# A fused streaming-encoder step: attention scores of a head pair on the two row halves of TensorE

## The chip, the cores and the metric

The kernel runs on one core of a Trainium2 chip. Its time is device microseconds (us) of one execution of the whole program. Of the runs shown the median is 2116.94 us (three runs, 2116.49 to 2117.7). TensorE multiplies and is the only writer of PSUM, VectorE (DVE) and ScalarE (ACT) read PSUM and work on SBUF, GpSimd (POOL) issues stores and does small SBUF work, and SP issues loads.

## The reference, cut to what matters

The reference is one layer of a conformer-like encoder on 1024 prompt frames and 64 sample frames, 1024 features, 16 heads of 64. What the change touches is the attention:

```python
h = rms_norm(x, norm_mix)
glu_a, glu_b, q, k, v, gates = jnp.split(h @ w_in, SPLITS, axis=-1)
# each frame attends to its own chunk of 64 and the 8 chunks before it, head by head (HEAD_DIM = 64)
sc = jnp.einsum("bnqhd,bnkhd->bnhqk", qc, band_k).astype(jnp.float32) * (dh ** -0.5)
sc = sc + rel_bias(rel_table, dist)
pr = jax.nn.softmax(sc, axis=-1).astype(v.dtype)
o = jnp.einsum("bnhqk,bnkhd->bnqhd", pr, band_v).reshape(b, s, h * dh)
```

Beside it stand a GLU, a causal depthwise convolution of width 31 with a layernorm, gates, an output projection, a channel mixer (up, convolution of width 3, GELU, down) and a per-layer input embedding.

## The kernel before

Features lie on the 128 partitions, frames along the free dimension. Each projection is a *job*: 128 output features of all 1088 frames, in three groups of 384, 384 and 320 columns. A product of float32 precision is made of three fp32r products: every operand is split into a high part (rounded to fp32r) and a low part (the rest), and high x high, high x low and low x high add up in PSUM (`mm3`, lines 154 to 166: eight blocks of the contraction, three matmuls each, so 24 matmuls a group). `split_into` (L168) makes the two parts: the high one with an ACT copy (L170), the low one with a DVE instruction (L171).

In the first long stage (up to about 916 us of the trace) the jobs follow each other in the order `order_1a`: for each of the eight pairs of heads i the jobs q, k, v, then three or four fill jobs (GLU value and gate, branch gates). The attention of pair i is threaded through those jobs. `job_group` calls `tick` twice a group: as the hook of `mm3`, after half of the 24 matmuls, and again after the group's evacuation `evac`. After a job's first group `w_ahead` splits the next job's weights (ACT L134, then DVE L135).

Attention works in 9 steps p a pair: 8 blocks of 128 queries against n = 128, 256, 384, 512 and then 640 keys, and one of the 64 sample queries against 576 keys. `pipe` has one entry a head and step, 18 for a pair, and each `tick` takes one:

- `step_S` (L463) computes the scores of one head. To use all 128 rows of the array with heads of 64 features, q and k are stored stacked: tile `Q[h]` holds the high part of q twice, `K[h]` the high part of k in one half of the partitions and the low part in the other, and `ql[h]` the low part of q over zeros. Two products (L481 with `Q`, L483 with `ql`) then give all three terms. 640 and 576 keys are done in two column halves. `tensor_tensor_reduce` (L487, DVE) adds the bias and takes the minimum, out of PSUM. The score tile has two PSUM banks, one buffer.
- `step_E` (L495, ACT) exponentiates and sums; one tick later DVE inverts the sum (L553) and `step_R` (L517, ACT) scales.
- `step_T` (L504) transposes the probabilities in blocks of 128 on TensorE, in another two PSUM banks, one buffer; ACT copies them out (L507).
- `step_PV` (L528) multiplies with v for both heads of a pair at once, head 0 on the left half of the array's columns and head 1 on the right half; `step_AT` splits the result and stores it.

Inside a tick the order on each engine is that of the program: `step_S`, `step_R` of the head before, background work, `step_PV`, `step_T`, `step_E`, background work. The background work (`bg_tick`) is the depthwise convolution's taps on DVE (L327), later the layernorm on DVE and ACT; a tick may do it in proportion to the TensorE time that it counts (`spent`, `RATIO`).

The evacuation of a q group is four ACT copies (L683) and two DVE instructions (L688), of 64 partitions each; that of a k group is two ACT copies (L696) and two DVE instructions (L708), and the cached keys take two and two (L601, L605). A projection has two PSUM buffers, so the group after the next one waits for this evacuation. PSUM's eight banks are: projections 2, scores 2, transposes 2, `o_ps` 1, small sums 1.

Of the kernel before, what the change touches and what calls it, by code (L numbers as in the profile page):

```python
# [9 lines left out]
F32 = mybir.dt.float32  # L10
# [65 lines left out]
def encoder_step(ctx: ExitStack, tc: tile.TileContext, I, O):  # L76
# [143 lines left out]
    with tc.manual_schedule():  # L220
# [55 lines left out]
        ps_s = att.enter_context(tc.tile_pool(name="ps_s", bufs=1, space=PSUM))  # L276
        ps_t = att.enter_context(tc.tile_pool(name="ps_t", bufs=1, space=PSUM))
# [4 lines left out]
        hsq = [at.tile([P, KW], F32, tag=f"K{h}", name="hsq") for h in range(2)]  # L282
# [174 lines left out]
        ql = [at.tile([P, T], F32R, tag=f"QL{h}", name="QL") for h in range(2)]  # L457
        for h in range(2):
            nc.gpsimd.memset(ql[h][64 - 64 * h:128 - 64 * h, :].bitcast(F32), 0.0)
        pipe = []  # L460
        stages = {"e": [], "t": [], "pv": []}

        def step_S(st):  # L463
# [11 lines left out]
            st.update(m=m, n=n, vb=(8 if smp else k0 // P), q0=q0)  # L475
# [9 lines left out]
            s = at.tile([P, 640], F32, tag="s", name="s", bufs=3)  # L485
            sm = at.tile([P, 3], F32, tag="sm", name="sm", bufs=6)
            nc.vector.tensor_tensor_reduce(  # L487
                out=s[0:m, 0:n].rearrange("p (x c) -> p x c", x=nh), in0=ps[0:m, 0:nh, 0:w],
                in1=c["bias"][h][0:m, b0:b0 + n].rearrange("p (x c) -> p x c", x=nh),
                scale=1.0, scalar=3e38, op0=ALU.add, op1=ALU.min, accum_out=sm[0:m, 0:1])  # L490
            st.update(s=s, sm=sm)

        def step_E(st):
            m, n, s, sm = st["m"], st["n"], st["s"], st["sm"]
            nc.scalar.activation(out=s[0:m, 0:n], in_=s[0:m, 0:n], func=AF.Exp, scale=-1.0, bias=sm[0:m, 0:1],  # L495
                                 accum_out=sm[0:m, 1:2])

        def step_T(st):
            m, n, s = st["m"], st["n"], st["s"]
            nb = (n + P - 1) // P  # L500
            ps = ps_t.tile([P, 1024], F32, tag="t", name="t_ps")
            for b in range(nb):
                w = min(P, n - b * P)
                nc.tensor.transpose(ps[0:w, b * P:b * P + m], s[0:m, b * P:b * P + w], ident[0:m, 0:m])  # L504
            pt = at.tile([P, 640], F32, tag="pt", name="pt", bufs=2)
            if m == P:
                nc.scalar.activation(out=pt[:, 0:n], in_=ps[:, 0:n], func=AF.Copy)  # L507
            else:
                nc.scalar.activation(out=pt[:, 0:512].rearrange("p (b q) -> p b q", q=P)[:, :, 0:m],
                                     in_=ps[:, 0:512].rearrange("p (b q) -> p b q", q=P)[:, :, 0:m], func=AF.Copy)  # L510
                nc.scalar.activation(out=pt[0:64, 512:512 + m], in_=ps[0:64, 512:512 + m], func=AF.Copy)
            st.update(pt=pt, nb=nb)

        def step_R(st):

            m, n, s, sm = st["m"], st["n"], st["s"], st["sm"]
            nc.scalar.activation(out=s[0:m, 0:n], in_=s[0:m, 0:n], func=AF.Copy, scale=sm[0:m, 2:3])  # L517

        def step_PV(pair):

            st = pair[0]
            c, m, n, nb = cur[st["i"]], st["m"], st["n"], st["nb"]
            o_ps = ps_o.tile([P, 512], F32, tag="o", name="o_ps")
            for b in range(nb):
                w = min(P, n - b * P)
                for x in pair:
                    a = 64 * x["h"]
                    nc.tensor.matmul(o_ps[a:a + 64, 0:m], lhsT=c["v"][0:w, st["vb"] + b, a:a + 64],  # L528
                                     rhs=x["pt"][0:w, b * P:b * P + m], start=(b == 0), stop=(b == nb - 1))
            st["o"] = o_ps  # L530

        def step_AT(st):
            m = st["m"]
            aT = at.tile([P, 2, P], F32R, tag="aT", name="aT")
            split_into(aT, 0, m, st["o"][:, 0:m])
# [4 lines left out]
        def tick(base=1.95):  # L540
# [3 lines left out]
            pair = len(stages["pv"]) == 2  # L544
            late = len(stages["t"]) > 1 or (stages["t"] and not pipe)
            if pair:
                spent += 0.218 * stages["pv"][0]["nb"] + 0.2
            if late:
                spent += 0.107 * ((stages["t"][0]["n"] + P - 1) // P)
            if pipe:  # L550
                spent += 0.5
            for x in stages["e"]:
                nc.vector.reciprocal(out=x["sm"][0:x["m"], 2:3], in_=x["sm"][0:x["m"], 1:2])  # L553
            new = pipe.pop(0) if pipe else None
            if new is not None:
                step_S(new)
            for x in stages["e"]:
                step_R(x)
            stages["e"].clear()
            bg_tick(RATIO * spent, 1)  # L560
            if pair:
                step_PV(stages["pv"])
                step_AT(stages["pv"][0])
                stages["pv"].clear()
            if late:
                st = stages["t"].pop(0)
                step_T(st)
                stages["pv"].append(st)
            if new is not None:
                step_E(new)  # L570
                stages["e"].append(new)
                stages["t"].append(new)
# [23 lines left out]
        def kv_cache(i):  # L596
            c = cur[i]
            kc = kc_t.pop(i)
            for h in range(2):
                a = 64 * h  # L600
                nc.scalar.activation(out=c["K"][h][a:a + 64, SEQ:SEQ + PAST], in_=kc[a:a + 64, 0:PAST], func=AF.Copy)  # L601
            for h in range(2):
                a, b = (0, 64) if h == 0 else (64, 0)
                kt = c["K"][h]
                nc.vector.tensor_tensor(out=kt[b:b + 64, SEQ:SEQ + PAST], in0=kc[a:a + 64, 0:PAST],  # L605
                                        in1=kt[a:a + 64, SEQ:SEQ + PAST].bitcast(F32), op=ALU.subtract)
# [14 lines left out]
        def job_begin(kind, i):  # L621
            hl = w_use()
            if kind == "q":
                cur[i] = {"Q": [at.tile([P, T], F32R, tag=f"Q{h}", name="Q") for h in range(2)]}
                kc_load(i)
                load_head(i)
            if kind == "k":
                if i < 7:
                    bias_rows(i + 1)
                cur[i]["K"] = [at.tile([P, KW], F32R, tag=f"K{h}", name="K") for h in range(2)]  # L630
# [17 lines left out]
        def evac(kind, i, g, ps):  # L648
# [28 lines left out]
                elif kind == "q":  # L677
                    c = cur[i]
                    for b in (0, 64):
                        for h in range(2):  # L680
                            a = 64 * h
                            o = a if b == 0 else 64 - a
                            nc.scalar.activation(out=c["Q"][h][o:o + 64, c0:c0 + n], in_=ps[a:a + 64], func=AF.Copy,  # L683
                                                 scale=-0.125)
                    for h in range(2):
                        a = 64 * h
                        q = c["Q"][h]
                        nc.vector.scalar_tensor_tensor(out=ql[h][a:a + 64, c0:c0 + n], in0=ps[a:a + 64],  # L688
                                                       scalar=-0.125, in1=q[a:a + 64, c0:c0 + n].bitcast(F32),
                                                       op0=ALU.mult, op1=ALU.subtract)  # L690
                elif kind == "k":
                    c = cur[i]
                    for h in range(2):
                        a = 64 * h
                        for o, w, d in segs(c0, n, 0, SEQ + PAST):
                            nc.scalar.activation(out=c["K"][h][a:a + 64, d:d + w], in_=ps[a:a + 64, o:o + w],  # L696
                                                 func=AF.Copy)
# [6 lines left out]
                    for h in range(2):  # L704
                        a, b = (0, 64) if h == 0 else (64, 0)
                        kt = c["K"][h]
                        for o, w, d in segs(c0, n, 0, SEQ + PAST):
                            nc.vector.tensor_tensor(out=kt[b:b + 64, d:d + w], in0=ps[a:a + 64, o:o + w],  # L708
                                                    in1=kt[a:a + 64, d:d + w].bitcast(F32), op=ALU.subtract)
                elif kind == "v":  # L710
# [21 lines left out]
                    if g == 2:  # L732
                        for p in range(9):
                            for h in range(2):
# [929 lines left out]
```

## Time and profile before

| what | value |
|---|---|
| median of the runs shown | 2116.94 us (2116.49 to 2117.7) |
| the profiled execution's own time | 2115.92 us |
| its span, first to last instruction | 2114.1 us |
| TensorE busy | 2078.1 us (98%) |
| VectorE busy | 1361.7 us (64%) |
| ScalarE busy | 881.6 us (42%) |
| granted TensorE clock, mean | 0.993 |
| share of TensorE in the chain that ended last | 88% |

The profile records every instruction of one execution. A matmul's row holds its time from start to modelled end; matmuls are pipelined, so the distance between the starts of two of them, not the duration, says what one costs. A wait is put down to the event that came last.

### The profile page before, as it was taken

To read this page: it belongs to the slowest core of one execution; us is meant where nothing else is said; L and a number is where in the kernel's file an instruction comes from. 1 tells how busy PE (TensorE), PEld (TensorE's weight loads), DVE (VectorE), ACT (ScalarE), POOL (GpSimd) and SP (SyncE) were. 2 spreads that over 40 slices of the span, in tenths; PEclk is the share of its full clock that TensorE was granted. 3 is DMA by queue.
4 is the path that set the end of the run, shared out by engine and by line. 5 is a ranking of instruction groups with operands and counts; after the bars stand their busy time and mean duration, and the time that the engine had idled before them with its cause. 6 is when DMAs were issued, how large, how long until landed. Compare 5 with 4: busy or idle time off the path is not lost.

```text
span 2114.1 us, 35321 instructions
## 1 busy us (share of the span) xinstructions
PE 2078.1 (98%) x14472; PEld 2024.5 (96%) x14472; DVE 1361.7 (64%) x2310; ACT 881.6 (42%) x1695; POOL 228.2 (11%) x455
## 2 busy tenths in 40 slices
PE   8999999999999999999999999999999999999997
PEld 6999999999999999899999998999999999999997
DVE  6887878777877755542354577777777753345644
ACT  5564737365746475850122344333333331123421
POOL 5110101111111011110000000000000020000400
PEclk9999999999999999999999999999999999999998
DMA  3313121212221321235343232121212173240011
GB/s 133 118 41 98 63 91 59 99 61 87 74 78 52 104 78 67 69 127 190 138 143 105 90 122 82 62 92 62 92 62 93 51 284 112 70 133 34 20 51 55
DMA packets 64705, 192.51 MB, mean 91 GB/s; under 512 B 8368, under 2 KB 22976, under 8 KB 63200
## 3 DMA queue, kind: packets, MB, share of 16 engines
q1 hardware_dynamic: 43072, 104.00, 14.6%
q0 software_dynamic: 21328, 85.71, 11.3%
q8 instruction: 113, 1.85, 0.4%
q10 hardware_dynamic: 144, 0.56, 0.1%
q14 instruction: 48, 0.39, 0.1%
HBM read 146.18 MB, written 54.01 MB: 95 GB/s over the span
## 4 chain that ended last, share of the span: by engine, by line
PE 88%; DVE 4%; ACT 4%; issue 2%; DMA 1%; POOL 0%; POOLq 0%; SPq 0%; DVEq 0%; ACTq 0%
PE pj L159 16%; PE pj L161 15%; PE pj L160 15%; PE pj L1173 7%; PE pj L1174 7%; PE pj L1172 7%; PE pj L1474 3%; PE pj L1475 3%; PE pj L1473 3%; PE o_ps L528 3%; PE t_ps L504 3%; PE s_ps L481 1%; PE s_ps L483 1%; DVE acc L1019 1%; ACT tmp L1018 0%
## 5 line engine op out<-in xcount | busy, mean ns | idle before, releaser
L159 PE MATMUL pj<-hT,whl 128*128 128x384 f32 (+1 forms) x1296 | 440.5, 340 | 3.6 <-DVE QL L688 2.2
L161 PE MATMUL pj<-hT,whl 128*128 128x384 f32 (+1 forms) x1296 | 424.9, 328 | 0.3 <-DVE whl L135 0.3
L160 PE MATMUL pj<-hT,whl 128*128 128x384 f32 (+1 forms) x1296 | 424.1, 327 | 0.0
L327 DVE SCALAR_TENSOR_TENSOR c<-u,cc,c 128x1118 f32<-128x1118 f32 x240 | 330.9, 1379 | 2.8
L159 PEld LDWEIGHTS pj<-hT,whl 128*128 128x128 f32 x1296 | 243.6, 188 | 8.6 <-issue 5.4
L161 PEld LDWEIGHTS pj<-hT,whl 128*128 128x128 f32 x1296 | 243.6, 188 | 0.6 <-DVE whl L135 0.6
L160 PEld LDWEIGHTS pj<-hT,whl 128*128 128x128 f32 x1296 | 243.9, 188 | 0.0
L1172 PE MATMUL pj<-mp,wq 128*128 128x272 f32 x704 | 204.0, 290 | 5.0 <-ACT ug L1248 2.7
L1174 PE MATMUL pj<-mp,wq 128*128 128x272 f32 x704 | 204.5, 290 | 0.0
L1173 PE MATMUL pj<-mp,wq 128*128 128x272 f32 x704 | 204.2, 290 | 0.0
L134 ACT ACTIVATE whl<-raw 128x1024 fp32r<-128x1024 f32 (+3 forms) x100 | 100.3, 1003 | 222.4 <-PE pj L1475 134.6
L1149 ACT ACTIVATE wq<-raw 128x512 fp32r<-128x512 f32 x144 | 84.2, 625 | 191.7 <-DVE raw L1158 135.6
L135 DVE TENSOR_TENSOR whl<-raw,whl 128x1024 fp32r<-128x1024 f32 (+3 forms) x100 | 115.7, 1158 | 62.5 <-ACT whl L134 62.1
L487 DVE CUSTOM_DVE_ANT_0 s<-s_ps,bias 128x640 f32<-128x640 f32 (+3 forms) x144 | 95.2, 661 | 81.5 <-PE s_ps L483 78.2
L1474 PE MATMUL pj<-gp,whl 128*128 128x384 f32 (+1 forms) x432 | 141.2, 327 | 0.3 <-DVE gp L1383 0.3
L1475 PE MATMUL pj<-gp,whl 128*128 128x384 f32 (+1 forms) x432 | 141.1, 327 | 0.0
L1473 PE MATMUL pj<-gp,whl 128*128 128x384 f32 (+1 forms) x432 | 141.0, 326 | 0.0
L1172 PEld LDWEIGHTS pj<-mp,wq 128*128 128x128 f32 x704 | 133.8, 190 | 5.4 <-ACT ug L1248 2.9
L1173 PE MATMUL pj<-bq,wq 128*128 128x272 f32 x480 | 138.5, 288 | 0.0
L1174 PE MATMUL pj<-bq,wq 128*128 128x272 f32 x480 | 138.3, 288 | 0.0
L1172 PE MATMUL pj<-bq,wq 128*128 128x272 f32 x480 | 138.1, 288 | 0.0
L1173 PEld LDWEIGHTS pj<-mp,wq 128*128 128x128 f32 x704 | 133.9, 190 | 0.0
(258 smaller groups left out, 4794.1 us busy)
## 6 DMA issues: line engine op xcount, KB each, us to landing
raw<-in_w_in SPq DMA_DIRECT2D x56, 512.0 KB, 3.2
raw<-in_w_ffn_up SPq DMA_DIRECT2D x44, 512.0 KB, 4.2
q_d<-ug POOLq DMA_DIRECT2D x22, 544.0 KB, 3.0
gp<-q_d POOLq DMA_DIRECT2D x22, 544.0 KB, 6.6
tg<-s_d POOLq DMA_DIRECT2D x16, 544.0 KB, 3.9
aP<-a_d POOLq DMA_DIRECT2D x8, 1088.0 KB, 6.0
a_d<-aT POOLq DMA_DIRECT2D x64, 128.0 KB, 2.2
f_d<-e_d POOLq DMA_DIRECT2D x16, 383.5 KB, 5.1
```

The lines of the kernel that those rows point to most:

```text
L134: nc.scalar.activation(out=hl[:, 0, 0:k, :], in_=raw[:, 0:k, :], func=AF.Copy)
L135: nc.vector.tensor_tensor(out=hl[:, 1, 0:k, :], in0=raw[:, 0:k, :], in1=hl[:, 0, 0:k, :].bitcast(F32), op=ALU.subtract)
L159: nc.tensor.matmul(ps, lhsT=wsel(hl, 0, k), rhs=r[:, 0, c0:c0 + n], start=(k == 0), stop=False)
L160: nc.tensor.matmul(ps, lhsT=wsel(hl, 0, k), rhs=r[:, 1, c0:c0 + n], start=False, stop=False)
L161: nc.tensor.matmul(ps, lhsT=wsel(hl, 1, k), rhs=r[:, 0, c0:c0 + n], start=False, stop=(k == K - 1))
L327: nc.vector.scalar_tensor_tensor(out=c_t[f], in0=u_t[f][:, j:j + CCOL], scalar=pc("conv_dw", f * CW + j), in1=c_t[f], op0=ALU.mult, op1=AL ...
L1172: nc.tensor.matmul(ps, lhsT=q[:, 0, kt, :], rhs=h, start=start and kt == 0, stop=False)
L1173: nc.tensor.matmul(ps, lhsT=q[:, 0, kt, :], rhs=l, start=False, stop=False)
L1174: nc.tensor.matmul(ps, lhsT=q[:, 1, kt, :], rhs=h, start=False, stop=stop and kt == 3)
L1473: nc.tensor.matmul(ps, lhsT=hl[:, 0, k, :], rhs=h, start=k == 0, stop=False)
L1474: nc.tensor.matmul(ps, lhsT=hl[:, 0, k, :], rhs=l, start=False, stop=False)
L1475: nc.tensor.matmul(ps, lhsT=hl[:, 1, k, :], rhs=h, start=False, stop=k == K - 1)
```

## The change

q and k are no longer stacked. `Q` and `K` are tiles of two planes, high and low, with head 0 on partitions 0 to 63 and head 1 on 64 to 127, as the projection leaves them; `ql` and its zeros are gone. The evacuation of q is `split_into` (one ACT copy, one DVE instruction on 128 partitions), that of k and of the cached keys one ACT copy and one DVE instruction for each stretch.

`step_S` now does both heads of a step. For each column half it issues three products (high x high, low x high, high x low) for each head, each with 64 rows of contraction: those of head 0 on the upper row half of the array, those of head 1 on the lower, alternating, into different PSUM banks. The scores of both heads take four banks. The transposes of both heads take the same four banks: scores and transposes are two tiles of one buffer (`tag="st"`, one buffer), so the scores of a step wait until the copies of the transposes before them are done, and the transposes wait until both reductions of the scores before them are done.

`pipe` has 9 entries a pair. Ticks alternate (`turn`): an even tick (the hook in a group's middle) does `step_S` of a new step, background work, `step_PV` of an older one, `step_E`; an odd tick (after a group's evacuation) does background work, `step_T` of both heads, the two inversions and the two `step_R` of the step just exponentiated. `spent` counts 1.1 for a pair's scores in place of 0.5 for a head's. During the start of the kernel the four banks belong to a pool `ps_h` that is closed before the first attention. The score tiles `s` in SBUF have four buffers in place of three.

```diff
@@ step_S
-            i, p, h = st["i"], st["p"], st["h"]
+            i, p = st["i"], st["p"]
...
-            ps = ps_s.tile([P, 2, 512], F32, tag="s", name="s_ps")
+            ps = ps_st[0].tile([P, 2, 2, 512], F32, tag="st", name="s_ps")
             wm = max(w, 256)
             for x in range(nh):
                 a = k0 + x * w
-                nc.tensor.matmul(ps[0:m, x, 0:wm], lhsT=c["Q"][h][:, q0:q0 + m], rhs=c["K"][h][:, a:a + wm],
-                                 start=True, stop=False)
-                nc.tensor.matmul(ps[0:m, x, 0:wm], lhsT=ql[h][:, q0:q0 + m], rhs=c["K"][h][:, a:a + wm],
-                                 start=False, stop=True)
...
+                for j, (sq, sk) in enumerate(((0, 0), (1, 0), (0, 1))):
+                    for h in range(2):
+                        r = slice(64 * h, 64 * h + 64)
+                        nc.tensor.matmul(ps[0:m, h, x, 0:wm], lhsT=c["Q"][r, sq, q0:q0 + m],
+                                         rhs=c["K"][r, sk, a:a + wm], start=(j == 0), stop=(j == 2))
+            st["s"], st["sm"] = [], []
+            for h in range(2):
+                s = at.tile([P, 640], F32, tag="s", name="s", bufs=4)
+                sm = at.tile([P, 3], F32, tag="sm", name="sm", bufs=6)
+                nc.vector.tensor_tensor_reduce(
+                    out=s[0:m, 0:n].rearrange("p (x c) -> p x c", x=nh), in0=ps[0:m, h, 0:nh, 0:w],
...
@@ step_T
-            ps = ps_t.tile([P, 1024], F32, tag="t", name="t_ps")
+            ps = ps_st[0].tile([P, 2, 1024], F32, tag="st", name="t_ps")
+            st["pt"] = []
+            for h, s in enumerate(st["s"]):
+                for b in range(st["nb"]):
+                    w = min(P, n - b * P)
+                    nc.tensor.transpose(ps[0:w, h, b * P:b * P + m], s[0:m, b * P:b * P + w], ident[0:m, 0:m])
+                pt = at.tile([P, 640], F32, tag="pt", name="pt", bufs=2)
+                if m == P:
+                    nc.scalar.activation(out=pt[:, 0:n], in_=ps[:, h, 0:n], func=AF.Copy)
...
@@ tick
+            odd = turn[0]
+            turn[0] = 1 - odd
+            new = done = flip = None
+            if not odd:
+                if pipe:
+                    new = pipe.pop(0)
+                    spent += 1.1
+                if stages["pv"]:
+                    done = stages["pv"].pop(0)
+                    spent += 0.218 * done["nb"] + 0.2
+            elif stages["t"]:
+                flip = stages["t"].pop(0)
+                spent += 0.214 * flip["nb"]
             if new is not None:
                 step_S(new)
             bg_tick(RATIO * spent, 1)
+            if done is not None:
+                step_PV(done)
             if new is not None:
                 step_E(new)
                 stages["e"].append(new)
+            if flip is not None:
+                step_T(flip)
+                stages["pv"].append(flip)
+            if odd:
+                for st in stages["e"]:
+                    for sm in st["sm"]:
+                        nc.vector.reciprocal(out=sm[0:st["m"], 2:3], in_=sm[0:st["m"], 1:2])
+                    step_R(st)
+                    stages["t"].append(st)
+                stages["e"].clear()
...
@@ evac, kind q
-                    for b in (0, 64):
-                        for h in range(2):
...
+                    split_into(c["Q"], c0, n, ps, scale=-0.125)
@@ evac, kind k
+                    kt = c["K"]
+                    for o, w, d in segs(c0, n, 0, SEQ + PAST):
+                        nc.scalar.activation(out=kt[:, 0, d:d + w], in_=ps[:, o:o + w], func=AF.Copy)
...
+                    for o, w, d in segs(c0, n, 0, SEQ + PAST):
+                        nc.vector.tensor_tensor(out=kt[:, 1, d:d + w], in0=ps[:, o:o + w],
+                                                in1=kt[:, 0, d:d + w].bitcast(F32), op=ALU.subtract)
...
         for p in range(9):
-                            for h in range(2):
-                                pipe.append({"i": i, "p": p, "h": h})
+                            pipe.append({"i": i, "p": p})
```

## Rows read from the trace of the kernel before

**Rows 1.** Page, part 1: busy time, share of the span, instructions of each engine

```profile
PE 2078.1 (98%) x14472; PEld 2024.5 (96%) x14472; DVE 1361.7 (64%) x2310; ACT 881.6 (42%) x1695; POOL 228.2 (11%) x455
```

**Rows 2.** Busy time by stretch: the attention, and the end of it

```profile
88.00:916.00 828.00, 820.09 (x5834) 780.75 (x5833) 601.51 (x969) 492.44 (x1049) 99.51 (x192) 1.00 0.22 74
...
855.00:915.00 60.00, 56.55 (x433) 51.09 (x432) 34.25 (x64) 52.13 (x91) 8.64 (x14) 1.00 0.17 57
```

**Rows 3.** TensorE in time, one tick: start, us, line, tiles, shape, count

```profile
340.14 0.31 PE L481 MATMUL s_ps<-K,Q 128*128 128x320 f32 x1
...
340.59 0.31 PE L483 MATMUL s_ps<-K,QL 128*128 128x320 f32 x1
340.83 1.09 PE L528 MATMUL o_ps<-pt,v 128*64 128x128 f32 x16
341.85 0.77 PE L504 MATMUL t_ps<-ident,s 128*128 128x128 f32 x5
342.37 0.39 PE L159 MATMUL pj<-hT,whl 128*128 128x320 f32 x1
342.60 0.31 PE L160 MATMUL pj<-hT,whl 128*128 128x320 f32 x1
```

**Rows 4.** First pair of PV products alone; then four weight loads of PV

```profile
340.83 0.33 PE L528 MATMUL o_ps<-pt,v 128*64 128x128 f32 x2
...
341.21 0.25 PEld L528 LDWEIGHTS o_ps<-pt,v 128*64 128x64 f32 x4
```

**Rows 5.** TensorE in time, scores of one head over 512 columns

```profile
330.04 0.39 PE L481 MATMUL s_ps<-K,Q 128*128 128x512 f32 x1
330.27 0.39 PE L483 MATMUL s_ps<-K,QL 128*128 128x512 f32 x1
```

**Rows 6.** TensorE in time, around instructions of 64 rows (the sample step)

```profile
373.74 0.34 PE L161 MATMUL pj<-hT,whl 128*128 128x384 f32 x1
374.00 0.52 PE L504 MATMUL t_ps<-ident,s 64*128 64x64 f32 x5
374.46 0.45 PE L159 MATMUL pj<-hT,whl 128*128 128x384 f32 x1
374.74 0.34 PE L160 MATMUL pj<-hT,whl 128*128 128x384 f32 x1
...
377.63 0.44 PE L159 MATMUL pj<-hT,whl 128*128 128x384 f32 x1
377.91 0.33 PE L160 MATMUL pj<-hT,whl 128*128 128x384 f32 x1
```

**Rows 7.** Groups by shape, 88 to 916: busy us, mean ns, idle before

```profile
L528 PEld LDWEIGHTS o_ps<-pt,v 128*64 128x64 f32 x1088 | 56.5, 136 | 19.5 <-issue 14.7 <-ACT pt L507 3.2 <-DVE sm L553 0.8
L517 ACT ACTIVATE s<-s,sm 128x640 f32<-128x640 f32 x64 | 52.9, 827 | 32.2 <-DVE sm L553 32.2
L507 ACT ACTIVATE pt<-t_ps 128x640 f32<-128x640 f32 x64 | 44.8, 700 | 14.4 <-PE t_ps L504 14.3
L481 PEld LDWEIGHTS s_ps<-K,Q 128*128 128x128 f32 x192 | 36.0, 188 | 1.3 <-DVE sm L487 1.3
L688 DVE SCALAR_TENSOR_TENSOR QL<-pj,Q 64x384 fp32r<-64x384 f32 x28 | 15.5, 555 | 37.2 <-ACT Q L683 36.9
```

**Rows 8.** All engines in time, a tick after a weight split

```profile
337.51 1.23 DVE L135 TENSOR_TENSOR whl<-raw,whl 128x1024 fp32r<-128x1024 f32 x1 [1.45 <-ACT whl L134]
337.61 0.60 PE L504 MATMUL t_ps<-ident,s 128*128 128x128 f32 x4
...
338.73 0.81 DVE L487 CUSTOM_DVE_ANT_0 s<-s_ps,bias 128x640 f32<-128x640 f32 x1
339.46 1.38 DVE L327 SCALAR_TENSOR_TENSOR c<-u,cc,c 128x1118 f32<-128x1118 f32 x1
```

**Rows 9.** Waits of TensorE's projections in 88 to 916: us, times, longest

```profile
PE pj L159 <- DVE QL L688: 2.2, 2, 1.6
...
PE pj L159 <- DVE K L708: 0.7, 1, 0.7
```

More of the change, by code (lines that the diff above doesn't have):

```diff
@@ L280, in encoder_step @@
         misc[0] = ps_m
-        hsq = [at.tile([P, KW], F32, tag=f"K{h}", name="hsq") for h in range(2)]
+        head = ExitStack()
+        ps_h = head.enter_context(tc.tile_pool(name="ps_h", bufs=1, space=PSUM))
+        ps_st = [None]
+        hsq2 = at.tile([P, 2, KW], F32, tag="K", name="hsq")
+        hsq = [hsq2[:, h] for h in range(2)]
         hd = {}
@@ L456, in encoder_step @@
         cur = {}
-        ql = [at.tile([P, T], F32R, tag=f"QL{h}", name="QL") for h in range(2)]
-        for h in range(2):
-            nc.gpsimd.memset(ql[h][64 - 64 * h:128 - 64 * h, :].bitcast(F32), 0.0)
         pipe = []
         stages = {"e": [], "t": [], "pv": []}
+        turn = [0]
         def step_S(st):
-            i, p, h = st["i"], st["p"], st["h"]
+            i, p = st["i"], st["p"]
             c = cur[i]
@@ L493, in step_E @@
         def step_E(st):
-            m, n, s, sm = st["m"], st["n"], st["s"], st["sm"]
-            nc.scalar.activation(out=s[0:m, 0:n], in_=s[0:m, 0:n], func=AF.Exp, scale=-1.0, bias=sm[0:m, 0:1],
-                                 accum_out=sm[0:m, 1:2])
+            m, n = st["m"], st["n"]
+            for s, sm in zip(st["s"], st["sm"]):
+                nc.scalar.activation(out=s[0:m, 0:n], in_=s[0:m, 0:n], func=AF.Exp, scale=-1.0, bias=sm[0:m, 0:1],
+                                     accum_out=sm[0:m, 1:2])
@@ L498, in step_T @@
         def step_T(st):
-            m, n, s = st["m"], st["n"], st["s"]
-            nb = (n + P - 1) // P
-            ps = ps_t.tile([P, 1024], F32, tag="t", name="t_ps")
[L502 to L511, printed above, removed]
@@ L514, in step_R, with step_PV @@
         def step_R(st):
[L516 to L521, printed above, removed]
+            m, n = st["m"], st["n"]
+            for s, sm in zip(st["s"], st["sm"]):
+                nc.scalar.activation(out=s[0:m, 0:n], in_=s[0:m, 0:n], func=AF.Copy, scale=sm[0:m, 2:3])
+        def step_PV(st):
             c, m, n, nb = cur[st["i"]], st["m"], st["n"], st["nb"]
@@ L525, in step_PV @@
                 w = min(P, n - b * P)
-                for x in pair:
-                    a = 64 * x["h"]
+                for h in range(2):
+                    a = 64 * h
                     nc.tensor.matmul(o_ps[a:a + 64, 0:m], lhsT=c["v"][0:w, st["vb"] + b, a:a + 64],
[L529 to L533, printed above, removed]
+                                     rhs=st["pt"][h][0:w, b * P:b * P + m], start=(b == 0), stop=(b == nb - 1))
             aT = at.tile([P, 2, P], F32R, tag="aT", name="aT")
-            split_into(aT, 0, m, st["o"][:, 0:m])
+            split_into(aT, 0, m, o_ps[:, 0:m])
             dma_st(out=a_d[st["i"]][:, :, st["q0"]:st["q0"] + m], in_=aT[:, :, 0:m].bitcast(F32))
@@ L543, in tick @@
             spent = base
[L544 to L554, printed above, removed]
+            odd = turn[0]
[11 more added lines that the diff above has]
+                spent += 0.214 * flip["nb"]
             if new is not None:
                 step_S(new)
-            for x in stages["e"]:
-                step_R(x)
-            stages["e"].clear()
             bg_tick(RATIO * spent, 1)
[L561 to L568, printed above, removed]
+            if done is not None:
+                step_PV(done)
             if new is not None:
@@ L598, in kv_cache @@
             kc = kc_t.pop(i)
-            for h in range(2):
[L600 to L606, printed above, removed]
+            kt = c["K"]
+            nc.scalar.activation(out=kt[:, 0, SEQ:SEQ + PAST], in_=kc[:, 0:PAST], func=AF.Copy)
+            nc.vector.tensor_tensor(out=kt[:, 1, SEQ:SEQ + PAST], in0=kc[:, 0:PAST],
+                                    in1=kt[:, 0, SEQ:SEQ + PAST].bitcast(F32), op=ALU.subtract)
         kc_t = {}
@@ L623, in job_begin @@
             if kind == "q":
-                cur[i] = {"Q": [at.tile([P, T], F32R, tag=f"Q{h}", name="Q") for h in range(2)]}
+                cur[i] = {"Q": at.tile([P, 2, T], F32R, tag="Q", name="Q")}
                 kc_load(i)
@@ L629, in job_begin @@
                     bias_rows(i + 1)
-                cur[i]["K"] = [at.tile([P, KW], F32R, tag=f"K{h}", name="K") for h in range(2)]
+                cur[i]["K"] = at.tile([P, 2, KW], F32R, tag="K", name="K")
                 kv_cache(i)
@@ L678, in evac @@
                     c = cur[i]
-                    for b in (0, 64):
[L680 to L690, printed above, removed]
+                    split_into(c["Q"], c0, n, ps, scale=-0.125)
                 elif kind == "k":
                     c = cur[i]
[L693 to L697, printed above, removed]
+                    kt = c["K"]
+                    for o, w, d in segs(c0, n, 0, SEQ + PAST):
+                        nc.scalar.activation(out=kt[:, 0, d:d + w], in_=ps[:, o:o + w], func=AF.Copy)
                     if g == 1:
@@ L808, in begin @@
             parts[g] = norm_parts([xt[f][:, c0:c0 + n] for f in range(KT)], "norm_mix", hd[g], n, hT, c0,
-                                  lambda: at.tile([P, 640], F32, tag="s", name="hn", bufs=3), HDVE[g])
-            two = ps_s.tile([P, 2, 512], F32, tag="s", name="pj") if g == 1 else None
+                                  lambda: at.tile([P, 640], F32, tag="s", name="hn", bufs=4), HDVE[g])
+            two = ps_h.tile([P, 2, 512], F32, tag="w", name="pj") if g == 1 else None
             for x, kind in enumerate(("gb", "ga")):
@@ L883, in encoder_step @@
         xt = None
+        head.close()
+        ps_st[0] = att.enter_context(tc.tile_pool(name="ps_st", bufs=1, space=PSUM))
         for kind, i in order_1a[2:-1]:
```

38 lines of the change are left out of this document (15 added, 23 removed).

## The prediction

> **What bounds the kernel now.** I read the page's part 1 first: TensorE is busy 98% of the span, the next engine 64% [rows 1]. Then the busy time by stretch: in the attention, 88 to 916 us, TensorE is busy 820.09 of 828 us at a granted clock of 1.00 (2.4 GHz), DVE 601.51, ACT 492.44 [rows 2]. So every us that TensorE's stream gets shorter or longer there is a us of the kernel, and a wait of another engine counts only where TensorE stands still. The exception is the end of the stage, 855 to 915, where ACT is busy 52.13 of 60 us and TensorE already loses 3.45 [rows 2]. Busy time does not say what a matmul costs, since matmuls overlap; so the third view is TensorE in time, where the reader takes distances between starts [rows 3 to 6].
>
> **The products: what is saved.** A score product of 320 columns follows the one before it after 0.15 us (340.14 to 340.59 is three distances), one of 512 after 0.23 [rows 3, 5]: 0.457 ns a column. A head has 256+256+384+512+4x640+576 = 4544 score columns in its nine steps (short steps are padded to 256). Before, a pair streams 2 heads x 2 products x 4544 columns = 8.31 us. After, it streams 3 products x 4544 = 6.23 us if the two heads run side by side. That is 2.08 us a pair, **-16.6 us** for eight.
>
> Do they run side by side? No row of before has two row halves at work. The nearest are the PV products, which use two column halves: the first two together take 0.33 us, hardly more than one score product's 0.31 [rows 4], and 16 of them, of some 0.27 us each, pass in 1.02 (340.83 to 341.85) [rows 3]. Their weight loads overlap too: four loads of 136 ns are through in 0.25 us [rows 4, 7], which is two distances of 0.11 apart plus one load. I take the same for row halves. The bounds: fully side by side as above, or one after the other, 12 products where 8 stood, which is 8.31 x 0.5 x 8 = +33.2 us in place of -16.6.
>
> **What is added: changes of the array's shape.** The sample step's transposes have 64 rows, and the rows around them show what it costs to leave the full array and to come back. From the last projection product (373.74) to the second one behind the transposes (374.74) pass 1.00 us; two products of 384 columns (0.175 each) and five short transposes (half of the 0.104 of a full one [rows 3], say 0.06 each) are 0.65 of it, so 0.35 is lost: 0.09 before the first transpose (0.26 instead of 0.175), 0.05 in its own start, and 0.21 on the way back, half of it in the first product, whose weights were not loaded ahead (374.46 to 374.74 is 0.28 instead of 0.175) [rows 6]. The same 0.28 stands behind a PV step that goes straight back to projections [rows 6]. Into PV it is 0.24 instead of 0.147 plus 0.05 [rows 3], 0.14; from PV to a transpose 1.02 - 8 x 0.109 - 0.05 for the entry, plus 0.055 in the first transpose, 0.155 in all [rows 3]. Full transposes after projections or scores of the full array, and back, cost nothing extra.
>
> So a score step on row halves, now entered from projections, costs about 0.20 to enter: 0.09 for the drain and 0.105 for a first load of 128 fp32r columns like the projections' (188 ns against 136 for PV's 64 columns [rows 7]). The bounds for it are 0.09 (drain alone) and 0.21 (the way back). Per pair of heads:
>
> - after: 9 entries into scores x 0.20, 7 score to PV x 0.14, 2 scores to projections (no PV yet) x 0.20, 2 projections to PV x 0.14, 9 PV to projections x 0.20, one visit to the sample's transposes 0.35: 1.80 + 0.98 + 0.40 + 0.28 + 1.80 + 0.35 = 5.61 us;
> - before: 9 entries into PV x 0.14, 8 PV to transposes x 0.155, the last PV to projections 0.20, the sample's transposes twice (one entered out of PV, so 0.21 + 0.35): 1.26 + 1.24 + 0.20 + 0.56 = 3.26 us.
>
> The difference is 2.35 us a pair, **+18.8 us** for eight. The halved scores sit between two changes each time, and before they were the same shape as the projections: that is why the saving is eaten.
>
> **Evacuations.** q falls from four ACT copies and two DVE instructions a group to one and one, k from two and two to one and one. TensorE waited 2.2 + 0.7 us in three places for the second of the two DVE instructions [rows 9]; without it each release comes 0.555 us earlier [rows 7]: **-1.7 us**. The rest of this relief is hidden under TensorE's stream.
>
> **The shared banks.** Now the transposes wait for both reductions of the step before, and the next scores for both copies. Queued behind a waiting transpose or score on TensorE stands the whole projection stream.
>
> *Scores to transposes.* The window is the PV step (1.02 to 1.3), the way back and 12 projection products (12 x 0.175 = 2.1): 3.3 us. Two reductions need 2 x 0.73 (338.73 to 339.46) and perhaps the rest of a convolution tap of 1.38 before them [rows 8]: 2.9. That fits by little. It does not always fit behind a weight split: there L135 stood idle 1.45 us for ACT's half and held the reduction back to 338.73, 1.1 us after the scores had streamed and the transposes behind them began (337.61) [rows 8]. In the new order two scalings of 0.83 [rows 7] stand ahead of ACT's half, and they wait for inversions that stand behind a tap. I count from the end of the transposes: a copy 0.7, two scalings 1.7, ACT's half 1.05, L135 1.22, 4.7 us; the scores end 3.2 after the same point; so the reductions start 1.5 late and need 1.5: 3.0 of 3.3, and a tap ahead of the inversions makes 4.4, 1.1 too many. Two such ticks a pair, 16 in all, between 0 and 1.1 each; I take a quarter us, as the tap is in front in some of them: **+4 us** (0 to 18).
>
> *Transposes to scores.* The window is 2.1 us (1.8 in a short group), two copies of 0.70 [rows 7] with ACT free take 1.4: hidden. At the end of the stage, where ACT has almost no slack [rows 2], a layernorm instruction in front makes it late; I allow four misses of half a us, **+2** (0 to 8; an allowance, not a row).
>
> **The sum**, against the profiled execution's 2115.92 us: -16.6 + 18.8 - 1.7 + 4 + 2 = +6.5, 2122.4. The median of the runs shown is 1.0 above that execution, so I say 2123.4, rounded to **2123 us**: 0.3% slower. A difference under 0.2% (4.2 us) can hardly be told from none here.
>
> **Rivals.**
>
> *Faster: entering the row halves costs only the drain.* If the first loads of both halves go on under the drain, each entry is 0.09 and not 0.20: 72 x 0.11 = -7.9; with that slack the shared banks may cost nothing: -6. Then 2109.5 us. For it: the short transposes' entry cost only 0.14 [rows 6]. Against: the return rows show a first load in the open every time [rows 6]. It decides from about 10.5 us below my sum on (below 2112.7); neither half alone does it.
>
> *No change.* The waits on the banks stay hidden and an entry costs what the transposes' did (0.14, -4.3): 2113 to 2121, middle 2117. For it: in the whole attention the scores' weight loads waited only 1.3 us for reductions [rows 7].
>
> *Slower: the loads of the two row halves go one after the other.* 188 against 136 ns for 128 and 64 columns is 0.81 ns a column [rows 7], so 0.104 a load and 0.208 a pair of loads, above the 0.147 of 320 columns, the 0.175 of 384 and the 0.117 of 256. Per pair of heads 24 x 0.061 + 3 x 0.033 + 6 x 0.091 = 2.1 us, +16.9: 2140. Against it: PV's loads overlap [rows 4].
>
> The Trainium skill, "TensorE: Matmul & The Clock Gate", section "Measured speedup vs the span model", has four row tiles run 3.07 times as fast as one after the other, not 4. No run here shows it yet. By that share two tiles would run 1.54 times as fast, an estimate from that page: twelve products of 12.46 us a pair would take 8.1, the saving would be 1.7 us and the sum 2138. I give it part of the chance of this rival, as PV's pairs show no such loss.
>
> *The change does not do what it says: the halves take turns.* Then 2123 + 49.8 = 2173 us. Against it: rows 4.
>
> **Chances.** My forecast (more than 0.2% slower, side by side) 0.40, no change 0.28, faster 0.20, loads in turn 0.08, halves in turn 0.04. So faster 0.20, same 0.28, slower 0.52. The range takes in the first four with the bank waits at half their upper bounds and leaves out the last: 2109 to 2141. The forecast's own range is 2119 to 2135.
>
> **What would show it.** In the new trace: six distances of about 0.147 us in a 640-key step of both heads, two products in each (right) or twelve (halves in turn) or six of 0.21 (loads in turn). A gap of 0.26 between the last projection product and the first score, and 0.28 in the first projection product behind PV, 18 times a pair where the latter stood twice or less. No wait for QL or K. Waits of transposes on the reduction (L487's new line) in the group behind a weight split, at most 1.1 us, and of scores on the copies near 900. The prediction is wrong if the waits on the shared banks come in every tick, since DVE is then the clock of the stage, or if the change of shape is not paid at all.

## The result and the profile after

The changed kernel takes 2202.1 us (median of six runs, 2199.4 to 2203.78), the kernel before in the same session 2116.72. The ratio is 1.0406, 95% interval 1.0391 to 1.042: 4.1% slower. The forecast was 2123 us, range 2109 to 2141. One of the six runs of the kernel before was slow (2868.01 us) and stands in that median, while the ratio compares fast runs alone. The direction was right; the time lies 61 us above the range, and none of the rivals gave it.

The page of the changed kernel, parts 1 and 4 (the counterpart of [rows 1]; in part 4 the shares of the chain that ended last):

```profile
span 2197.3 us, 35659 instructions
PE 2094.6 (95%) x14696; PEld 2012.2 (92%) x14696; DVE 1320.1 (60%) x2246; ACT 829.8 (38%) x1583; POOL 224.2 (10%) x453
...
PE 82%; ACT 7%; DVE 5%; issue 4%; DMA 1%; POOL 0%; SPq 0%; POOLq 0%; ACTq 0%; DVEq 0%
```

TensorE has 16.5 us more of busy time, but the span is 83.2 us longer: TensorE stands still, which it hardly did before. No other engine is busier than before. The busy time by stretch says where, with the attention now ending at 1003 us (counterpart of [rows 2]; columns: stretch, its length, busy us and instructions of PE, PEld, DVE, ACT, POOL, granted clock, DMA share, GB/s):

```profile
88.00:1003.00 915.00, 841.93 (x6078) 772.19 (x6078) 564.92 (x914) 448.04 (x952) 99.60 (x193) 0.99 0.20 67
```

This stretch is 87 us longer than that of [rows 2], and idle time of TensorE in it rose from 7.91 to 73.07 us. Who is waited for stands in the waits of TensorE from 88 to 1010 us (the counterpart of [rows 9]; waiting line, what it waits for, us in total, times, longest):

```profile
PE t_ps L511 <- ACT pt L514: 66.8, 64, 4.4
PE t_ps L511 <- ACT pt L519: 5.1, 8, 0.6
PE v_ps L708 <- ACT lnb L384: 1.2, 2, 0.6
PE pj L159 <- ACT sg L677: 0.7, 1, 0.7
```

64 + 8 is 72, the number of steps: in every step, once, the transposes wait for ACT's copy of transposes, 71.9 us in all. No wait of TensorE's products for q, k, a reduction or the scores' banks is left. One step in time shows which copy it is (all engines' rows of the two lines; the last column is the idle time before and its releaser):

```profile
364.08 0.60 PE L511 MATMUL t_ps<-ident,s 128*128 128x128 f32 x4
...
364.78 0.60 ACT L514 ACTIVATE pt<-t_ps 128x512 f32<-128x512 f32 x1
...
365.43 0.66 PE L511 MATMUL t_ps<-ident,s 128*128 128x128 f32 x4 [0.75 <-ACT pt L514]
...
366.18 0.60 ACT L514 ACTIVATE pt<-t_ps 128x512 f32<-128x512 f32 x1 [0.81 <-PE t_ps L511]
```

The first four transposes are head 0's. Its copy runs from 364.78 to 365.38, and head 1's transposes start 0.05 after it. It is the copy of the *same step*, not of the step before. `step_T` takes one tile of four banks for both heads, and in the program's order head 0's copy out of that tile stands ahead of head 1's transposes into it.

The score and PV products of the tick before, which belong to the two neighbouring steps (counterpart of [rows 3]):

```profile
359.72 0.34 PE L161 MATMUL pj<-hT,whl 128*128 128x384 f32 x1
359.99 1.14 PE L485 MATMUL s_ps<-K,Q 64*128 64x320 f32 x12
361.06 0.88 PE L536 MATMUL o_ps<-pt,v 128*64 128x128 f32 x12
361.86 0.45 PE L159 MATMUL pj<-hT,whl 128*128 128x384 f32 x1
362.15 0.34 PE L160 MATMUL pj<-hT,whl 128*128 128x384 f32 x1
```

Twelve products of 320 columns pass in 1.07 us (359.99 to 361.06). Their starts, from the trace, come in six pairs: 359.987 and 359.991, 360.236 and 360.243, 360.385 and 360.387, and so on, 1 to 7 ns within a pair and some 0.145 us from one pair to the next, except the first distance of 0.25. The entry is 0.27 instead of 0.175, and 0.29 passes between the first two projection products behind PV. The prediction had named 0.147, 0.26 and 0.28.

For the whole kernel, the distances from each product's start to the next start, summed by the tile that the first of them writes (us, worked out from the traces; two experiments stand beside):

```
         before    after    transposes first   tile per head
pj       1855.5   1863.2        1866.6            1859.7
s_ps       71.9     63.5          63.6              67.3
o_ps       73.4     69.1          69.6              70.3
t_ps       52.5    142.0          53.6              53.7
```

The transposes alone have 89.5 us more, 1.24 in each of 72 steps on average. The other three together have 5.0 less than before.

Part of the loss is TensorE's clock. [rows 2] had a granted clock of 1.00 in the attention, and so has "transposes first" below (88 to 917 us). In the changed kernel five stretches of the attention, 17 us in all, show 0.50, which is 1.2 GHz. Each begins within one of the transposes' longest waits or at most 0.8 us behind its end (1.87 to 4.40 us; four other waits of 1.92 to 2.24 us have no such stretch). All six runs show it in the mean granted clock, 0.987 to 0.990, where those of "transposes first" have 0.992 to 0.995. One of the five stretches, as a stretch of the view of [rows 2] and as rows in time:

```profile
926.20:929.60 3.40, 3.40 (x12) 3.40 (x12) 0.00 (x0) 2.60 (x4) 0.00 (x0) 0.50 0.16 53
...
926.06 0.64 PE L511 MATMUL t_ps<-ident,s 128*128 128x128 f32 x2 [1.88 <-ACT pt L514]
...
927.13 0.52 PE L161 MATMUL pj<-hT,whl 128*128 128x384 f32 x1
927.45 0.52 PE L159 MATMUL pj<-hT,whl 128*128 128x384 f32 x1
```

A projection product of 384 columns follows the one before it after 0.32 us there, instead of 0.175. For 17 us that is some 8 us of the loss, an estimate from these distances. The idle time in the waits is the main part, 71.9 us.

### The profile page after: what moved, and what is told of

It reads as the page before. It is cut to its first block, busy times and chain, and to the rows that moved or that the text cites. A ratio compares the mean times of both kernels' runs of the same rounds, so it can differ in the third digit from the quotient of the medians.

```text
span 2197.3 us, 35659 instructions
## 1 busy us (share of the span) xinstructions
PE 2094.6 (95%) x14696; PEld 2012.2 (92%) x14696; DVE 1320.1 (60%) x2246; ACT 829.8 (38%) x1583; POOL 224.2 (10%) x453
## 4 chain that ended last, share of the span: by engine, by line
PE 82%; ACT 7%; DVE 5%; issue 4%; DMA 1%; POOL 0%; SPq 0%; POOLq 0%; ACTq 0%; DVEq 0%
PE pj L159 15%; PE pj L161 14%; PE pj L160 14%; PE pj L1159 7%; PE pj L1160 7%; PE pj L1158 7%; PE pj L1461 3%; PE pj L1460 3%; PE pj L1459 3%; PE o_ps L536 2%; PE t_ps L511 2%; PE s_ps L485 2%; ACT pt L514 2%; ACT s L501 1%; DVE c L329 1%
## 5 line engine op out<-in xcount | busy, mean ns | idle before, releaser
L491 DVE CUSTOM_DVE_ANT_0 s<-s_ps,bias 128x640 f32<-128x640 f32 (+3 forms) x144 | 90.4, 664 | 145.2 <-PE s_ps L485 145.0
L511 PE MATMUL t_ps<-ident,s 128*128 128x128 f32 (+2 forms) x560 | 86.7, 277 | 71.9 <-ACT pt L514 66.8
L511 PEld LDWEIGHTS t_ps<-ident,s 128*128 128x128 f32 (+2 forms) x560 | 61.9, 141 | 92.0 <-ACT pt L514 82.5
L1158 PEld LDWEIGHTS pj<-mp,wq 128*128 128x128 f32 x704 | 134.1, 191 | 5.4 <-ACT ug L1234 2.9
L1159 PE MATMUL pj<-bq,wq 128*128 128x272 f32 x480 | 138.6, 289 | 0.0
L1160 PE MATMUL pj<-bq,wq 128*128 128x272 f32 x480 | 138.3, 288 | 0.0
```

The costliest lines, as they stand in the source:

```text
L511: nc.tensor.transpose(ps[0:w, h, b * P:b * P + m], s[0:m, b * P:b * P + w], ident[0:m, 0:m])
L1158: nc.tensor.matmul(ps, lhsT=q[:, 0, kt, :], rhs=h, start=start and kt == 0, stop=False)
L1159: nc.tensor.matmul(ps, lhsT=q[:, 0, kt, :], rhs=l, start=False, stop=False)
L1160: nc.tensor.matmul(ps, lhsT=q[:, 1, kt, :], rhs=h, start=False, stop=stop and kt == 3)
```

## The experiments

**Two theories.** A: the loss is the wait of head 1's transposes for head 0's copy, and it is there because one tile serves both heads while the copy stands between their transposes; taking either away gives back all of it. B: ACT is late in the new order of ticks, or four shared banks are too tight, so that a wait taken from one place returns at another.

**Transposes first.** The order inside `step_T` changes, the tile stays.

```diff
                     nc.tensor.transpose(ps[0:w, h, b * P:b * P + m], s[0:m, b * P:b * P + w], ident[0:m, 0:m])
+            for h in range(2):
                 pt = at.tile([P, 640], F32, tag="pt", name="pt", bufs=2)
```

> All transposes of a step (both heads) are issued before its two copies; nothing else is changed. Theory A (head 1's transposes wait for head 0's copy, because that copy stands before them in program order and reads the tile that they write): the 71.9 us of waits of transposes on the copies are gone, with the matmul tails in them 87 us; time 2202 - 87 = 2115, range 2108 to 2126. Theory B (ScalarE is late in the two-tick scheme, the copies would be late in any order): the wait moves to the next scores, time 2180 or more. My forecast's own sum for this kernel without that wait was 2123.

Measured: 2117.22 us (2115.55 to 2118.26) beside 2117.45 for the kernel before, ratio 0.9999 (0.999 to 1.0008). TensorE's waits in the attention:

```profile
PE s_ps L485 <- ACT pt L515: 5.6, 6, 2.4
PE t_ps L511 <- DVE sm L491: 3.4, 9, 0.8
```

The wait between the heads is gone, the granted clock in the attention is back at 1.00, and 85 us are gone with them. What comes back elsewhere is 9.0 us, in the two places that the prediction had named. Theory B would have had to show tens of us here.

**A tile per head.** The order stays as in the change, with the copy between the heads; the four banks are two tiles of two banks.

```diff
-            ps = ps_st[0].tile([P, 2, 1024], F32, tag="st", name="t_ps")
+            ps = [ps_st[0].tile([P, 1024], F32, tag=f"st{h}", name="t_ps") for h in range(2)]
```

(The same for `s_ps`, and `ps[h]` for `ps[:, h]`. This also splits the waits between steps by head.)

> The order of the changed kernel is kept (transposes of head 0, copy, transposes of head 1, copy), but scores and transposes of each head have a two-bank tile of their own in place of one four-bank tile. Theory A in its narrow form (the wait is set because both heads' transposes are one tile, though they lie in different banks): the wait is gone as in the first kernel, 2115 (2108 to 2126). If the order alone makes the wait, whatever the tiles: 2202, with the same 72 waits. Theory B: 2180 or more.

Measured: 2113.08 us (2112.21 to 2114.98), ratio 0.9979 (0.997 to 0.9988); run once more later, 2114.21 (2111.96 to 2115.93), 0.9985 (0.9976 to 0.9994). This and the next are the fastest versions found, about 0.2% under the kernel before. Of the shared banks' waits one is left in its trace:

```profile
PE s_ps L485 <- ACT pt L514: 4.9, 8, 1.8
```

As the order of the copy is untouched here and ACT has the same work, neither ACT's speed nor the number of banks was the cause. Theory A holds. The 4.1 us under "transposes first" are as much as the waits are shorter (4.9 instead of 9.0).

**Both edits together.**

> Transposes first and a tile for each head. Theory A: nothing is left to gain from the second edit, within 4 us of the first kernel. If waits of scores on the second copy or of transposes on the second reduction are left in the first kernel, this takes away those of head 0: up to 8 us less.

Measured: 2113.97 us (2110.39 to 2115.46), ratio 0.9981 (0.9972 to 0.999), with the same 4.9 us of waits. The two edits take away the same thing.

**Heads in turn within a column half** (on "transposes first"): the three products of head 0 are issued ahead of the three of head 1.

```diff
-                for j, (sq, sk) in enumerate(((0, 0), (1, 0), (0, 1))):
-                    for h in range(2):
+                for h in range(2):
+                    for j, (sq, sk) in enumerate(((0, 0), (1, 0), (0, 1))):
```

> The first kernel (transposes first), with the score products of head 0 all ahead of those of head 1 in each column half, so that no two neighbours lie on different row halves except at the border. If the row halves save what the trace of the changed kernel shows (pairs 1 to 8 ns apart, 0.146 us a pair of 320 columns): 6 products in turn in place of 3 pairs, 12.46 in place of 6.23 us a pair of heads, +49.8 less the few neighbours at the borders that still overlap: 40 to 50 us over the first kernel, 2155 to 2165. If the overlap is an artefact of the records: no difference.

Measured: 2118.06 us, ratio 1.0 (0.9991 to 1.0009); the scores' distances sum to 64.7 us against 63.6. I had meant this to take the side-by-side work away, and it didn't: the starts still come in pairs, now 3 to 20 ns apart (361.058 and 361.068, 361.307 and 361.317). So the price of side by side had to be tried in another way.

**Heads in turn over a whole step** (on "a tile per head"): six products of head 0, of both column halves, ahead of six of head 1.

```diff
-            for x in range(nh):
-                a = k0 + x * w
-                for j, (sq, sk) in enumerate(((0, 0), (1, 0), (0, 1))):
-                    for h in range(2):
-                        r = slice(64 * h, 64 * h + 64)
+            for h in range(2):
+                r = slice(64 * h, 64 * h + 64)
+                for x in range(nh):
+                    a = k0 + x * w
+                    for j, (sq, sk) in enumerate(((0, 0), (1, 0), (0, 1))):
```

> Base: a tile per head (2113.1). Here all six score products of head 0, of both column halves, are issued ahead of the six of head 1. Theory A (a row half starts its products as soon as it is free, however they are ordered): at 640 keys the two heads still run side by side, the start distances of the scores stay near 67 us in all and the time stays within 6 us of 2113. Theory B (the overlap reaches only about three products ahead): a step of 640 keys pays up to 0.88 us more (three pairs of 0.146 us, two column halves, run one after the other); with 36 such steps at most about +32, so 2113 to 2145.

Measured: 2125.8 us (2124.57 to 2127.84), ratio 1.004 (1.0026 to 1.0054): 12 us over its base, and the scores' distances grew by 12.5 (79.8 against 67.3). That is 0.31 in each of the 40 steps with two column halves (the expectation says 36, a slip). One step of 640 keys, with the copies out of the two heads' tiles before it:

```profile
353.66 1.30 ACT L514 ACTIVATE pt<-t_ps 128x640 f32<-128x640 f32 x2
...
356.15 1.54 PE L485 MATMUL s_ps<-K,Q 64*128 64x320 f32 x12
357.62 0.33 PE L536 MATMUL o_ps<-pt,v 128*64 128x128 f32 x2
```

It is 1.47 us to the first PV, where 1.07 is side by side and some 2.0 would be one after the other. In the trace the first product of head 1 (the seventh issued, known by its weight load, which waits for head 1's own tile) starts at 356.555, beside the third (356.548), and head 0's sixth, which releases its reduction, only at 356.983. Head 1's tile had been free since 354.96, so it is not that wait that sets the start. In 37 of the 40 steps the seventh starts beside the third, so it passed three products issued ahead of it. That is the reach of Theory B and lies between the two limits; what sets it is open.

**Heads apart** (on "a tile per head"): `step_S` is called for head 0 ahead of the background work and PV, and for head 1 behind PV.

```diff
-                step_S(new)
+                step_S(new, 0)
             bg_tick(RATIO * spent, 1)
             if done is not None:
                 step_PV(done)
             if new is not None:
+                step_S(new, 1)
                 step_E(new)
```

> Base: a tile per head (2113.1). Here the scores of head 0 of the next step are issued ahead of the projections' product and PV of the present one, and those of head 1 behind it, so no two heads stand side by side. If the side-by-side products are what pays for the shape changes: the saving of 5.5 us in each of 8 pairs is lost (+44), and there are some 56 more visits of a shape at 0.2 (+11), together about 2168 (2145 to 2185). If side by side saves nothing: only the visits, about 2124.

Measured: 2171.34 us (2170.69 to 2172.14), ratio 1.0254 (1.0238 to 1.027), 58 us over its base where 55 were worked out.

```profile
362.01 1.14 PE L485 MATMUL s_ps<-K,Q 64*128 64x320 f32 x6
363.08 1.09 PE L534 MATMUL o_ps<-pt,v 128*64 128x128 f32 x16
```

Six products of one head alone take 1.07 us to the first PV, exactly what twelve of both heads took above. So the second head's products are free side by side. Six distances of 0.145 are 0.87 of the 1.07 us, and the other 0.20 is what the prediction paid for one more visit. In the whole kernel the scores' distances grew by 51.5 us (118.8 against 67.3). The transposes' grew by 9.0 (62.7 against 53.7): they wait for DVE's reductions and inversions again, 7.0 us in twelve waits, which the 55 didn't hold. That the totals are so near is partly luck.

**Two steps' PV together** (on "a tile per head"), to halve the changes from scores to PV: PV waits until two steps are transposed, with four buffers for `pt`, and the two results share the bank of `o_ps`.

```diff
-                if stages["pv"]:
-                    done = stages["pv"].pop(0)
-                    spent += 0.218 * done["nb"] + 0.2
+                if len(stages["pv"]) == 2 or (stages["pv"] and not (new or stages["e"] or stages["t"])):
+                    done = list(stages["pv"])
+                    stages["pv"].clear()
+                    spent += 0.218 * sum(x["nb"] for x in done) + 0.2
```

> Base: a tile per head (2113.1). Here the PV of two steps stand together, so that half of the visits from scores to PV fall away: 36 x 0.14 us = 5 us less. Expected 2108 (2103 to 2114), if nothing behind it comes late; if the probabilities of the first step of the two are held too long, the scores wait for a buffer and the time goes to 2113 to 2125.

Measured: 2127.6 us (2122.98 to 2128.32), ratio 1.0041 (1.0029 to 1.0054): 14 us slower than its base. PV's distances fell by 4.0 us (70.3 to 66.3; 5 were hoped for), but those of the projections rose by 12.5, where the waits behind them lie:

```profile
PE s_ps L485 <- ACT pt L514: 6.8, 10, 2.8
PE t_ps L511 <- DVE sm L491: 6.4, 7, 1.8
```

In this trace the granted clock was also 0.50 for 13.6 us of the attention, in that of the base for 3.4; reckoned as above, some 5 us of the loss are the clock. The rest is not: the fastest of the five runs, 2122.98 us at a mean granted clock of 0.994 as in the base, is still 10 us over it.

A step without PV, in time:

```profile
113.77 1.04 ACT L134 ACTIVATE whl<-raw 128x1024 fp32r<-128x1024 f32 x1
...
114.85 1.23 DVE L135 TENSOR_TENSOR whl<-raw,whl 128x1024 fp32r<-128x1024 f32 x1 [2.29 <-ACT whl L134]
...
115.99 0.82 DVE L491 CUSTOM_DVE_ANT_0 s<-s_ps,bias 128x640 f32<-128x640 f32 x1
...
116.97 0.63 PE L511 MATMUL t_ps<-ident,s 128*128 128x128 f32 x4 [0.54 <-DVE sm L491]
```

DVE stands idle 2.29 us for ACT's half of a weight split, and the first reduction starts 3.0 us after the scores (112.98). The transposes come after twelve projection products alone, without the 1.0 to 1.2 us of PV in between, and wait.

**The same with the background work spread evenly.** It could also have been that a doubled PV draws twice the convolution's taps into one tick, ahead of the reductions.

```diff
+                if stages["pv"]:
+                    spent += 0.218 * stages["pv"][-1]["nb"] + 0.2
                 if len(stages["pv"]) == 2 or (stages["pv"] and not (new or stages["e"] or stages["t"])):
                     done = list(stages["pv"])
                     stages["pv"].clear()
-                    spent += 0.218 * sum(x["nb"] for x in done) + 0.2
```

> Two steps' PV together as before, but the VectorE and ScalarE work that is spread over the steps is allotted by each step's own PV and no longer all at once in the step that issues two. Theory A (the loss of 14 us came from that work being bunched ahead of the reductions): the waits of the transposes for the reductions (6.4 us and the gaps they leave in the projections) go, and the time is about 2109 (2106 to 2113). Theory B (the loss comes from the missing PV itself, whose 1.1 us stood between scores and transposes and gave the reductions time behind a weight split): the waits stay and the time stays near 2127 (2120 to 2130).

Measured: 2132.14 us (2131.08 to 2133.81), ratio 1.0071 (1.0057 to 1.0085). Bunched taps are not the cause. The transposes still wait for reductions (4.1 us, seven times). The scores' waits for copies doubled to 13.1, and the time lies above the range of Theory B too; why is open. That the missing PV is the cause is argued from rows like those above and not shown by a run of its own.

> The tile per head once more, on the chip of the run beside it: 2113 (2110 to 2116), 0.2% under the kernel before.

This is the second run of "a tile per head" told above.

## Why the prediction was wrong

- **The failed step** stands in "The shared banks": "Now the transposes wait for both reductions of the step before, and the next scores for both copies." That list has the waits between steps and misses the one *inside* `step_T`. Both heads' transposes write one tile, and head 0's copy is issued between them. The new step was costed as ten transposes in a row. The numbers to size it stood in the rows: 72 steps, each at least one copy (0.70 for 640 columns [rows 7]) long and uncovered, since the projections stand behind the waiting transposes; with the shorter copies of the shorter steps that alone is some 40 us, an estimate from the rows of before. The trace shows 71.9 us of idle time and 89.5 us of distances, and a granted clock of 0.50 behind some of the longest waits. The prediction's own sign of being wrong, waits on the shared banks in every tick, comes nearest, but it named DVE, and the wait is for ACT. Two edits, one of the order and one of the tiles, take this wait away and bring the kernel to 2117.2 and 2113.1.
- **Side by side, and its price.** Right: pairs of starts some ns apart, 0.27 at the entry, 0.29 behind PV. The rivals "loads in turn" and "halves in turn" fall. The Trainium skill's "TensorE: Matmul & The Clock Gate", section "Measured speedup vs the span model", from which the estimate of 1.54 was worked out, has its figure for four row tiles. The estimate doesn't hold for two row halves here: six products of one head and twelve of both take the same 1.07 us.
- **Evacuations** (-1.7). Right in kind, too small: the waits for QL and K are gone, and by the distances they had cost 5.2 us. The three waits of [rows 9] went whole and not by 0.555 each, and so did eight of some 0.2 us behind k groups that the prediction had not seen.
- **Scores to transposes** (+4, at most 1.1 each). Without the failed step: 3.4 us in nine waits, at most 0.8. **Transposes to scores** (+2, of 0 to 8): 5.6 in six. In the change itself neither shows; each step is 1.2 us longer there, which fits.
- **The sum without the failed step.** 2123.4 was forecast, 2117.2 measured with "transposes first", 6 too many. The distances between starts in the traces of the kernel before and of "transposes first" tell where (us, worked out from the traces; for the first line each distance is replaced by the median of the distances between the same two kinds of product, so that waits drop out, and the other lines are what goes beyond these medians):

```
                                            forecast   measured
products and changes of shape                 +2.2       +0.8
evacuations of q and k                        -1.7       -5.2
waits for the shared banks                    +6.0      +11.5
two waits of before that were not credited     0.0       -6.9
```

  So the price of the row halves, -16.6 + 18.8, was right within 1.4 us. The 6 too many are waits of the kernel before that the change removed, less what the shared banks took beyond the forecast. The two that were not credited are scores that waited for the reduction before them, and PV that waited for copies (idle time alone, 88 to 916 us of the kernel before):

```profile
PE s_ps L481 <- DVE sm L487: 2.0, 3, 1.0
PE o_ps L528 <- ACT pt L507: 2.0, 4, 0.9
```

- **The direction** came out as forecast, but for another reason: the forecast's sum, put right, is a kernel that can't be told from the one before.

## What to carry to other kernels

When two independent parts come to share one PSUM tile, write down the program's order of all writes into it and reads out of it, also inside the step, before costing anything: in this kernel a read of the first part issued ahead of the writes of the second was a wait, even though the banks differ. Give each part its own tile, or issue all writes first; either takes a few lines, and here it was worth 85 us. A wait of TensorE can cost more than its own length: here the granted clock was 0.50 behind some of the longest. And a piece of work on the engine that bounds the kernel may be the cover for another engine's latency: two PV steps taken together saved 4 us of TensorE's own time and lost 14 in all, some 5 of them by the clock.

## What was not expected of the hardware

TensorE started score products of the two row halves out of the order in which they were issued. With three products of one half issued ahead of three of the other, they still started in pairs 3 to 20 ns apart, where two of the same half follow each other after 0.145 us. With six ahead of six, the seventh started at 356.555, before head 0's sixth at 356.983. The Trainium skill's "TensorE: Matmul & The Clock Gate", section "Step-by-step: what each phase is for", says that matmuls stay in program order and only weight loads are pulled ahead; the traces of these two runs differ, and they decide.
